# Contrast adjustment on one core: the first store in three pieces beside the loads, and a quarter of the fourth store on another queue

## The chip, the core and the metric

The kernel runs on one core of one Trainium2 chip. The metric is the device time of one execution in microseconds (us); the median of several runs counts.

## The reference

For each image and colour channel (48 planes of 512 x 512 float32 numbers) the mean is taken, and every number is moved away from it by a factor of 1.5 and clipped to 0..1:

```
mean = np.mean(x, axis=(2, 3), keepdims=True)
return np.clip(mean + factor * (x - mean), 0, 1).astype(np.float32)
```

50.33 MB are read and 50.33 MB are written, once each.

## The kernel before

The input is seen as 6 tiles of 128 rows with `ROW` = 16384 numbers (64 KB) each, 8 MB a tile. One plane fills 16 rows, so a tile holds 8 planes. A ring of three such tiles lies in the core's memory (`BUFS` = 3): tile t uses slot t % 3, and load 3 can only start when store 0 has left slot 0, load 4 when store 1 has landed, load 5 when store 2 has.

What is done for a tile:

- **load** (L77): SyncE's queue (SPq in the profile) brings the tile in. Tile 0 comes in three parts (1, 3 and 4 MB), tile 2 in two (7.25 MB and a tail of 0.75 MB, `TAIL`), the others whole.
- **sum_up** (L96) with **add** (L84): row sums. ScalarE runs a copy in place that also sums (L88); for tiles 0 to 2 VectorE sums the first 4352 columns (`SUM`, L91) and ScalarE the rest. For tiles 3 to 5 ScalarE does it alone. Tile 0 is summed by halves.
- **clip** (L101): TensorE multiplies the sums by `blockw` (L105), which adds the 16 rows of a plane and scales, so `bias` holds each row's shift. VectorE then does two operations in place: multiply and add (L108), then clip to 0..1 (L111). Given `cuts`, it does so piece by piece.
- **store** (L80): stores of tiles 0 to 2 go out on ScalarE's queue (ACTq), those of tiles 3 to 5 on SyncE's.

Each queue issues its instructions in the order of the program, and a DMA that waits holds up what is queued behind it on that engine. The order is written out by hand (`manual_schedule`, L115 to L141). On SyncE: the loads of tiles 0, 1 and 2, then load 3 (waiting for store 0), load 4 (store 1), load 5 (store 2), then stores 3, 4 and 5. On ScalarE: the sums of tile 0, the sum of tile 1, store 0 in two pieces (1 MB and 7 MB), the sum of tile 2, store 1, store 2, the sums of tiles 3, 4 and 5. On VectorE: the sums and clips in the order of the tiles. A dependency put in by hand (L125) makes the first piece of store 0 wait for the large part of load 2.

Of the kernel before, what the change touches and what calls it, by code (L numbers as in the profile page):

```python
# [1 line left out]

# [4 lines left out]


P = 128  # L10
ROW = 16384
HALF = ROW // 2
BUFS = 3
SHORT = 2048
SUM = 4352
TAIL = 1536


@with_exitstack
def kernel(  # L20
    ctx: ExitStack,
    tc: tile.TileContext,
    x: bass.AP,
    factor: float,
    out: bass.AP,
):

    nc = tc.nc  # L30
    f32 = mybir.dt.float32
    Alu = mybir.AluOpType
    Act = mybir.ActivationFunctionType

    B, C, H, W = x.shape
    n_img, n_pix = B * C, H * W
    ppi = n_pix // ROW
    per_tile = P // ppi
    n_tiles = n_img // per_tile
    assert ppi * ROW == n_pix and per_tile * n_tiles == n_img  # L40

    factor = float(factor)
    wconst = (1.0 - factor) / float(n_pix)

    x_f = x.rearrange("b c h w -> (b c h w)")
    out_f = out.rearrange("b c h w -> (b c h w)")

    def dram(ap, t, c0=0, c1=ROW):
        return bass.AP(tensor=ap.tensor, offset=t * P * ROW + c0, ap=[[ROW, P], [1, c1 - c0]])

    consts = ctx.enter_context(tc.tile_pool(name="consts", bufs=1))
    xpool = ctx.enter_context(tc.tile_pool(name="xpool", bufs=1))
    small = ctx.enter_context(tc.tile_pool(name="small", bufs=1))
    psum = ctx.enter_context(tc.tile_pool(name="psum", bufs=1, space=bass.MemoryType.PSUM))


    sums = small.tile([P, 4 * n_tiles], f32, name="sums")
    bias = psum.tile([P, n_tiles], f32, name="bias")

    blockw = consts.tile([P, P], f32, name="blockw")  # L60
    blocks = blockw.rearrange("p (a b) -> p a b", b=ppi)
    nc.gpsimd.memset(blockw, wconst)  # L62
    for base, step in ((0, -ppi), (ppi - 1, ppi)):
        nc.gpsimd.affine_select(  # L64
            out=blocks,
            in_=blocks,
            compare_op=Alu.is_ge,
            fill=0.0,
            base=base,
            pattern=[[step, per_tile], [0, ppi]],  # L70
            channel_multiplier=1 if step < 0 else -1,
        )


    ring = xpool.tile([P, BUFS, ROW], f32, name="ring")

    def load(t, c0=0, c1=ROW):  # L77
        return nc.sync.dma_start(out=ring[:, t % BUFS, c0:c1], in_=dram(x_f, t, c0, c1))  # L78

    def store(t, c0=0, c1=ROW):  # L80
        queue = nc.scalar if t < BUFS else nc.sync
        return queue.dma_start(out=dram(out_f, t, c0, c1), in_=ring[:, t % BUFS, c0:c1])  # L82

    def add(t, col, c0, c1, c2):  # L84
        xt = ring[:, t % BUFS, :]
        own = sums[:, 4 * t + col : 4 * t + col + 2]
        part = xt[:, c1:c2]
        nc.scalar.activation(out=part, in_=part, func=Act.Copy, accum_out=own[:, 0:1])  # L88
        if c0 == c1:
            return [own[:, 0:1]]  # L90
        nc.vector.tensor_reduce(  # L91
            out=own[:, 1:2], in_=xt[:, c0:c1], axis=mybir.AxisListType.X, op=Alu.add
        )
        return [own[:, 0:1], own[:, 1:2]]

    def sum_up(t):  # L96
        if t == 0:
            return add(t, 0, 0, SUM, HALF) + add(t, 2, HALF, HALF + SUM, ROW)
        return add(t, 0, 0, SUM if t < BUFS else 0, ROW)

    def clip(t, parts, *cuts):  # L101
        xt = ring[:, t % BUFS, :]
        shift = bias[:, t : t + 1]
        for k, part in enumerate(parts):
            nc.tensor.matmul(shift, blockw, part, start=k == 0, stop=k == len(parts) - 1)  # L105
        for c0, c1 in zip((0, *cuts), (*cuts, ROW)):
            part = xt[:, c0:c1]
            nc.vector.tensor_scalar(  # L108
                out=part, in0=part, scalar1=factor, scalar2=shift, op0=Alu.mult, op1=Alu.add
            )  # L110
            nc.vector.tensor_scalar(  # L111
                out=part, in0=part, scalar1=0.0, scalar2=1.0, op0=Alu.max, op1=Alu.min
            )

    with tc.manual_schedule():  # L115
        load(0, 0, SHORT)
        load(0, SHORT, HALF)
        load(0, HALF, ROW)
        load(1)
        most = load(2, 0, ROW - TAIL)  # L120
        load(2, ROW - TAIL, ROW)
        clip(0, sum_up(0), SHORT)
        parts = sum_up(1)
        first = store(0, 0, SHORT)
        tc.add_manual_dep(  # L125
            first.ins,
            most.ins.name,
            mybir.DependencyInfo(mybir.DependencyClass.Sync, mybir.DependencyReason.DATA),
            reason="the first store follows the loads",
        )  # L130
        store(0, SHORT, ROW)
        clip(1, parts)
        parts = sum_up(2)
        store(1)
        clip(2, parts)
        store(2)
        for t in range(BUFS, n_tiles):
            load(t)
        for t in range(BUFS, n_tiles):
            clip(t, sum_up(t))  # L140
            store(t)  # L141


# [1 line left out]
_INS = ['x', 'factor']  # L145
_OUTS = [((16, 3, 512, 512), 'float32')]

_NUMBERS = {'factor': 1.5}


# [26 lines left out]
```

## Time and profile before

| | us |
|---|---|
| median of 3 runs | 241.26 |
| lowest, highest of the runs | 241.06, 244.25 |
| the profiled execution, its own time | 242.66 |
| span of that execution in the profile | 240.9 |
| VectorE busy, in the span | 123.6 |
| ScalarE busy, in the span | 70.8 |
| share of the 16 DMA engines, SyncE's queue (q1) | 73.9% |
| share of the 16 DMA engines, ScalarE's queue (q10) | 24.4% |

One execution was profiled. Its times are counted from the first instruction of the span. DVE is VectorE, ACT is ScalarE, SP is SyncE; SPq and ACTq are these engines as issuers of DMAs. "Landing" is the end of a transfer as its semaphore shows it. In the windows, the columns after the stretch and its length are the busy us of PE, PEld, DVE, ACT and POOL with their instructions, then TensorE's clock, the mean busy share of the DMA engines, and the GB/s moved. In the timeline, a line gives start, duration, engine, source line and operation, and in brackets the idle time before it.

### The profile page before, as it was taken

The page shows a single profiled execution, that of the slowest core. Times are in us where ns is not written, and L with a number is a line of the kernel's source. Part 1 is how long each engine was busy: PE and PEld are TensorE (multiplying, and loading weights), DVE is VectorE, ACT ScalarE, POOL GpSimd, SP SyncE. Part 2 cuts the span into 40 slices and gives each one's busy share as a digit, 9 for nine tenths or more (in the row PEclk, how much of TensorE's full clock was granted, in tenths as well). Part 3 has the DMA queues.
Part 4 walks back from the last instruction along what each step waited for, and adds up shares of the span by engine and source line. Part 5 has one row for each costly group of instructions (what it writes and reads, how often), then busy time and mean ns, then how long its engine had stood idle before and what let it go on. Part 6 is the DMA issues. An engine that isn't in the chain of part 4 may idle for free.

```text
span 240.9 us, 167 instructions
## 1 busy us (share of the span) xinstructions
PE 6.3 (3%) x22; PEld 5.4 (2%) x22; DVE 123.6 (51%) x18; ACT 70.8 (29%) x15; POOL 1.1 (0%) x7
## 2 busy tenths in 40 slices
PE   0010100010001000000000000000000000000000
PEld 0010100010000000000000000000000000000000
DVE  0072899949998995000000059930089949950000
ACT  2052300960790000000009930029907950000000
POOL 1000000000000000000000000000000000000000
DMA  7999989979999899999999999889899898989894
GB/s 297 411 430 441 511 348 506 473 335 404 501 457 457 348 348 435 435 435 435 424 446 413 446 413 457 381 326 522 348 348 522 348 522 348 522 348 511 359 511 185
DMA packets 2304, 100.66 MB, mean 418 GB/s; under 512 B 256, under 2 KB 256, under 8 KB 384
## 3 DMA queue, kind: packets, MB, share of 16 engines
q1 hardware_dynamic: 1728, 75.50, 73.9%
q10 hardware_dynamic: 576, 25.17, 24.4%
HBM read 50.33 MB, written 50.33 MB: 418 GB/s over the span
## 4 chain that ended last, share of the span: by engine, by line
DMA 54%; ACT 16%; DVE 14%; another core or an unknown queue 3%; SPq 1%; PE 0%; issue 0%; ACTq 0%
DMA ring<-in_x_dram 45%; ACT ring L88 16%; DMA out_dram<-ring 9%; DVE ring L108 7%; DVE ring L111 7%; SPq L78 1%; PE bias L105 0%; ACTq L82 0%; ACTq L172 0%
## 5 line engine op out<-in xcount | busy, mean ns | idle before, releaser
L88 ACT ACTIVATE ring<-ring 128x16384 f32<-128x16384 f32 (+2 forms) x7 | 68.8, 9834 | 124.5 <-DMA ring<-in_x_dram 124.5
L108 DVE TENSOR_SCALAR ring<-ring,bias 128x16384 f32<-128x16384 f32 (+2 forms) x7 | 52.8, 7538 | 72.5 <-PE bias L105 71.7
L111 DVE TENSOR_SCALAR ring<-ring 128x16384 f32<-128x16384 f32 (+2 forms) x7 | 52.3, 7475 | 0.2
L91 DVE TENSOR_REDUCE sums<-ring 128x1 f32<-128x4352 f32 x4 | 18.7, 4683 | 18.0 <-DMA ring<-in_x_dram 18.0
L105 PE MATMUL bias<-sums,blockw 128*128 128x1 f32 x22 | 6.3, 360 | 190.5 <-ACT ring L88 186.0
L105 PEld LDWEIGHTS bias<-sums,blockw 128*128 128x128 f32 x22 | 5.4, 313 | 191.2 <-ACT ring L88 169.9
L88 ACT ACT_TABLE_LOAD x1 | 1.3, 1283 | 0.8 <-PEq L158 0.8
L88 ACT ACTIVATION_READ_ACCUMULATOR ring<-ring 128x1 f32 x7 | 1.3, 186 | 0.0
L64 POOL TENSOR_SCALAR_AFFINE_SELECT blockw<-blockw 128x128 f32<-128x128 f32 x2 | 0.7, 340 | 0.1
L62 POOL MEMSET blockw<- 128x128 f32 x1 | 0.2, 204 | 0.3 <-POOLq L158 0.3
L158 POOL MEMSET const-bfloat16-1.0<- 128x1 bf16 x1 | 0.1, 101 | 0.0
L158 POOL MEMSET const-uint8-127<- 128x1 uint8 x1 | 0.1, 101 | 0.0
L158 POOL MEMSET const-float32-0.0<- 128x1 f32 x1 | 0.1, 98 | 0.3 <-issue 0.3
L158 POOL MEMSET const-float32-1.0<- 128x1 f32 x1 | 0.1, 98 | 0.0
## 6 DMA issues: line engine op xcount, KB each, us to landing
ring<-in_x_dram SPq DMA_DIRECT2D x1, 7424.0 KB, 56.6
out_dram<-ring ACTq DMA_DIRECT2D x1, 7168.0 KB, 20.7
ring<-in_x_dram SPq DMA_DIRECT2D x1, 4096.0 KB, 20.9
ring<-in_x_dram SPq DMA_DIRECT2D x1, 3072.0 KB, 11.7
ring<-in_x_dram SPq DMA_DIRECT2D x1, 1024.0 KB, 4.9
out_dram<-ring ACTq DMA_DIRECT2D x1, 1024.0 KB, 4.3
ring<-in_x_dram SPq DMA_DIRECT2D x1, 768.0 KB, 58.0
ring<-in_x_dram SPq DMA_DIRECT2D x4, 40.7
```

Of the source, the lines that this page charges most:

```text
L62: nc.gpsimd.memset(blockw, wconst)
L64: nc.gpsimd.affine_select(out=blocks, in_=blocks, compare_op=Alu.is_ge, fill=0.0, base=base, pattern=[[step, per_tile], [0, ppi]], channel ...
L78: return nc.sync.dma_start(out=ring[:, t % BUFS, c0:c1], in_=dram(x_f, t, c0, c1))
L88: nc.scalar.activation(out=part, in_=part, func=Act.Copy, accum_out=own[:, 0:1])
L91: nc.vector.tensor_reduce(out=own[:, 1:2], in_=xt[:, c0:c1], axis=mybir.AxisListType.X, op=Alu.add)
L105: nc.tensor.matmul(shift, blockw, part, start=k == 0, stop=k == len(parts) - 1)
L108: nc.vector.tensor_scalar(out=part, in0=part, scalar1=factor, scalar2=shift, op0=Alu.mult, op1=Alu.add)
L111: nc.vector.tensor_scalar(out=part, in0=part, scalar1=0.0, scalar2=1.0, op0=Alu.max, op1=Alu.min)
L158: nc = _bacc.Bacc("TRN2", target_bir_lowering=False, num_devices=1)
```

## The change

- Load 2 comes in one part; the dependency of the first store on it is taken out.
- Tile 0 is clipped in three pieces (2048, 6144 and 8192 columns; 8, 24 and 32 KB a row), and each piece is stored on ScalarE's queue.
- The order on ScalarE changes: all three pieces of store 0 come before the sum of tile 1, and store 1 before the sum of tile 2.
- Tile 3 is clipped in two pieces (4096 and 12288 columns). The first, a quarter, is stored from ScalarE's queue ahead of the sum of tile 4; the rest stays on SyncE's queue behind load 5.

```diff
-TAIL = 1536
+QUARTER = ROW // 4
...
-    def store(t, c0=0, c1=ROW):
-        queue = nc.scalar if t < BUFS else nc.sync
-        return queue.dma_start(out=dram(out_f, t, c0, c1), in_=ring[:, t % BUFS, c0:c1])
+    def store(queue, t, c0=0, c1=ROW):
+        queue.dma_start(out=dram(out_f, t, c0, c1), in_=ring[:, t % BUFS, c0:c1])
...
-        most = load(2, 0, ROW - TAIL)
-        load(2, ROW - TAIL, ROW)
-        clip(0, sum_up(0), SHORT)
-        parts = sum_up(1)
-        first = store(0, 0, SHORT)
-        tc.add_manual_dep(
-            first.ins,
-            most.ins.name,
-            mybir.DependencyInfo(mybir.DependencyClass.Sync, mybir.DependencyReason.DATA),
-            reason="the first store follows the loads",
-        )
-        store(0, SHORT, ROW)
-        clip(1, parts)
-        parts = sum_up(2)
-        store(1)
-        clip(2, parts)
-        store(2)
+        load(2)
+        clip(0, sum_up(0), SHORT, HALF)
+        store(nc.scalar, 0, 0, SHORT)
+        store(nc.scalar, 0, SHORT, HALF)
+        store(nc.scalar, 0, HALF, ROW)
+        for t in range(1, BUFS):
+            clip(t, sum_up(t))
+            store(nc.scalar, t)
         for t in range(BUFS, n_tiles):
             load(t)
-        for t in range(BUFS, n_tiles):
+        clip(BUFS, sum_up(BUFS), QUARTER)
+        store(nc.scalar, BUFS, 0, QUARTER)
+        store(nc.sync, BUFS, QUARTER, ROW)
+        for t in range(BUFS + 1, n_tiles):
             clip(t, sum_up(t))
-            store(t)
+            store(nc.sync, t)
```

## The prediction

> **What bounds the kernel now.** I read the page first, then the chain of work that ended last, then busy time by windows, then the timeline of the stretch that is edited.
>
> The page's slices and packet line:
>
> ```profile
> DMA  7999989979999899999999999889899898989894
> DMA packets 2304, 100.66 MB, mean 418 GB/s; under 512 B 256, under 2 KB 256, under 8 KB 384
> ```
>
> The 16 DMA engines are busy in nearly every slice, while VectorE is busy for 51% of the span and ScalarE for 29%. The chain of waits agrees: it runs from transfer to transfer.
>
> ```profile
> 60.10 20.70 DMA out_dram<-ring
> ...
> 80.89 45.76 DMA ring<-in_x_dram
> ...
> 158.81 23.32 DMA ring<-in_x_dram
> ```
>
> The reader should see that load 3 leaves at 80.89, as the first store lands at 80.80, and that it takes 45.76 us because store 1 runs beside it: sharing costs a transfer time but wastes no bytes. How fast the bytes move is in the windows (last columns: DMA share, GB/s):
>
> ```profile
> 0.00:2.00 2.00, 0.00 (x0) 0.00 (x0) 0.00 (x0) 1.20 (x1) 1.09 (x7) 1.00 0.17 25
> 58.00:64.00 6.00, 0.00 (x0) 0.00 (x0) 5.96 (x2) 2.55 (x1) 0.00 (x0) 1.00 1.09 459
> 84.00:92.00 8.00, 0.00 (x0) 0.00 (x0) 7.97 (x2) 0.00 (x0) 0.00 (x0) 1.00 1.01 336
> 92.00:156.00 64.00, 0.59 (x2) 0.50 (x2) 16.51 (x3) 13.95 (x2) 0.00 (x0) 1.00 1.00 433
> 156.00:164.00 8.00, 0.00 (x0) 0.00 (x0) 2.78 (x1) 2.82 (x1) 0.00 (x0) 1.00 0.98 393
> 176.00:182.00 6.00, 0.00 (x0) 0.00 (x0) 6.00 (x1) 0.00 (x0) 0.00 (x0) 1.00 1.02 350
> 182.00:238.00 56.00, 0.58 (x2) 0.50 (x2) 28.71 (x4) 13.95 (x2) 0.00 (x0) 1.00 0.99 431
> 238.00:240.90 2.90, 0.00 (x0) 0.00 (x0) 0.00 (x0) 0.00 (x0) 0.00 (x0) 1.00 0.00 0
> ```
>
> Loads and stores mixed (92 to 156) give 433 GB/s, stores alone (182 to 238) 431. At 433, 100.66 MB take 232.5 us; the span is 240.9, so 8.4 us are lost. Each window's loss is its length times (1 - rate/433): 1.9 us at the start, 1.8 at 84 to 92, 0.7 at 156 to 164, 1.2 at 176 to 182, 2.9 at the end; sum 8.5. Start and end stay. So 3.7 us is all that any new order of these bytes can win, and an added loss must be a new stretch in which the engines starve or run slowly.
>
> **The change part by part.** The stretch that is edited first:
>
> ```profile
> 28.05 1.29 DVE L108 TENSOR_SCALAR ring<-ring,bias 128x2048 f32<-128x2048 f32 x1 [0.68 <-PE bias L105]
> 29.38 1.23 DVE L111 TENSOR_SCALAR ring<-ring 128x2048 f32<-128x2048 f32 x1
> 30.52 7.68 DVE L108 TENSOR_SCALAR ring<-ring,bias 128x14336 f32<-128x14336 f32 x1
> 38.24 7.63 DVE L111 TENSOR_SCALAR ring<-ring 128x14336 f32<-128x14336 f32 x1
> ...
> 59.63 1.55 ACTq L82 DMA_DIRECT2D out_dram<-ring  x2
> ```
>
> The first piece is ready at 30.6 and leaves at 59.63, held by the wait on load 2.
>
> *VectorE.* From 2048 and 14336 columns, the first operation costs 0.227 us + 0.520 ns a column, the second 0.160 us + 0.521 ns. One cut more costs 0.39 us. The pieces of tile 0 are ready at 30.6, 37.4 (6144 columns: 3.42 + 3.36) and 46.3. Tile 3's cut makes its end 159.2 instead of 158.8, but that store lies behind load 5 on SyncE's queue until about 182: nothing. Its quarter is ready at 141.3 + 2.36 + 2.29 = 146.0.
>
> *Issues.* There are 17 DMAs instead of 16: load 2 loses one, store 0 and store 3 gain one each. An issue takes 0.33 to 1.08 us of its queue, hidden under the transfers queued before it; bare, it would be that.
>
> *ScalarE's queue, which now waits for VectorE.* Queued behind store 0's third piece is tile 1's sum; its pass starts at 42.03 today and would start at 46.3 + 0.4 to 1.1 = 46.7 to 47.4. The matmul and VectorE's clip of tile 1 wait for it: 10.42 to the sum's end, 1.1 to the clip (52.41 to 53.53), 17.5 for the clip, so store 1 leaves at 75.8 to 76.5 instead of 71.11. Tile 2's sum now stands behind store 1: 10.4 more, 1.1, 17.5, and store 2 leaves near 105.5 instead of 93.93. What hides this: loads 0 to 2 and store 0 are 33.55 MB, 77.5 us at 433, so the engines have work until 1.9 + 77.5 = 79.4. Store 1 needs about 1 us from issue to first bytes (the first load is issued at 0.80, and 0 to 2 moves 25 GB/s), so 1.9 to 2.6 us are spare. Store 2 joins behind store 1, whose landing releases load 4 at 119.6: 14 us spare. With the cover gone each us late is a us of idle engines.
>
> *Load 1 and load 2.* Store 0 now shares the engines with them. Load 1 can be late by 4.7 us free (its reader is held until 46.7). Load 3 still waits for the end of store 0, which is the end of the same 33.55 MB: near 80, as now. Removing the wait on load 2's large part and its separate 0.75 MB tail moves nothing else.
>
> *How the sharing starts.* A queue that joins a running one has two rows. The old first piece joined at 60 us beside the end of load 2: 459 GB/s at 58 to 64, no loss. Load 3 joined store 1 near 84: 1.8 us lost. The new join, near 32, is the old piece in direction and size, but the other queue has megabytes left, as near 84. Bounds 0 to +1.8 (less than 0 is excluded, that stretch runs at 426 or more already); between rows that are equally near I take the middle, +0.9.
>
> *The quarter of store 3.* 2 MB, 4.8 us of the engines, leaves ScalarE's queue at 146 behind store 2. Today store 2 lands at about 158.8 and releases load 5, with load 4 ending at 161.15 and store 3 behind load 5. So the engines run dry there, 0.7 us lost. The quarter fills this. Bounds 0 to -0.7; I take -0.7, as 4.8 us of work lies ready.
>
> *The tail.* The quarter goes ahead of load 5's last packets, so load 5 lands at 182.13 + 4.8 - 0.7 = 186.2. From landing to the issue of store 5 take the row of today, 214.29 - 182.13 = 32.2, plus 1 for first bytes: 33.2. The work queued meanwhile is 6 MB of store 3 and 8 MB of store 4, 14.5 + 19.4 = 33.9 (today 38.7). 0.7 us is spare, where 5.5 was: cost 0, up to +1 if load 5's last engine is late. Store 4 leaves near 195 for a need at 200: nothing.
>
> Sum: +0.9 - 0.7 + 0 = +0.2. The profiled execution took 242.66 (span 240.9 and 1.76 around it), so it would take 242.9. It lies 1.4 above the median of 241.26 of the runs; the median plus 0.2 gives 241.5.
>
> **Two rules weighed.** The row for small transfers here is 459 GB/s while the old 1 MB piece ran. The Trainium skill, "DMA: Bandwidth & Descriptors", section "Bandwidth", gives 341 GB/s for a lone 1 MB transfer and wants at least 1 MiB; it speaks against cutting the store, and by it the first piece would cost 1.05 MB/341 - 1.05 MB/433 = +0.65 us (an estimate), where the row beside other work says 0. The row for two queues is 433 GB/s at 92 to 156 against 431 from one queue. The same page, section "Issuing engines are not separate DMA queues", says a second issuing engine saves issue time only; by it the quarter on ScalarE's queue is worth about 0, and what the trace adds is the order behind load 5 that a second queue escapes.
>
> **The rivals.**
> 1. *The bytes set the end, and join and filled gap nearly cancel:* 240.6 to 242.4, likeliest 241.5. For it: 64 us of mixed traffic at 433. Chance 0.48.
> 2. *The early join costs the full 1.8 us and the gap is not filled:* slower, 241.26 + 1.8 = 243.1. It decides as soon as the join costs more than the filled gap gives, 0.7. For it: 84 to 92; against: 58 to 64. Chance 0.20.
> 3. *Store 5 becomes late:* if load 5's landing slips by one 64 KB packet of every engine (19.4/8 = 2.4 us), the 0.7 spare leaves 1.7: 243.0. Against: all engines have equal bytes before load 5. Chance 0.12.
> 4. *The stalls go:* the gap is filled, the new join is free, and load 3, joining a queue already mixed, no longer stalls: 241.26 - 0.7 - 1.8 = 238.8. Against: store 1 runs there alone as before. Chance 0.15.
> 5. *The wait on ScalarE's queue dries the engines:* store 1 over 5 us later than worked out, past 81; then 2 to 4 us idle, some 246 at the worst. Against: the spare 1.9 to 2.6. Chance 0.05.
>
> **How the numbers follow.** 241.5 is the first case. 239.5 to 244.2 takes in the first three and most of the fourth, leaving out half of it (0.08), the fifth (0.05) and 0.05 of the second and third beyond 244.2. About 2% is what a measurement can tell from no change: under 236.4 lies beyond even the 3.7 us (237.6) but for noise, 0.02; over 246.1 the worst of the fifth and double mishaps, 0.06; between them 0.92.
>
> **What would show it.** Right: stores on ScalarE's queue at about 30.7, 37.4 and 46.3; tile 1's sum at 47; store 1 at 76; load 3 still issued at 79 to 82; 156 to 164 near 433; store 5 issued near 218.5; last store about 19.4 us. Wrong: a window under 400 GB/s between 30 and 50 above 1.8 us of loss; engines idle before store 1; a gap before store 5; load 3 issued far from 80, which would say that the queues do not share as I take it.

## The result and the profile after

The changed kernel takes 240.26 us (median; 239.29 to 240.85), the kernel before, in a larger set of runs, 241.58 us (240.79 to 244.28). The ratio is 0.9928, 95% interval 0.9904 to 0.9951: 1.7 us gained (1.2 to 2.3). The ratio is taken over the runs; the two medians lie 1.3 us apart, which is inside its interval. The forecast was 241.5, a gain of nothing. The time lies inside the range of 239.5 to 244.2, but the interval leaves no doubt of a gain, and the +0.2 of the sum pointed the other way.

The profiled execution of the changed kernel took 239.29 us, with a span of 237.5, against 242.66 and 240.9. It is the fastest of its runs, so a difference of these two profiles shows places, not sizes. The page's slices and packet line:

```profile
DMA  7999989999999998989898998989997999999894
DMA packets 2448, 100.66 MB, mean 424 GB/s; under 512 B 272, under 2 KB 272, under 8 KB 272
```

The same bytes move, at 424 GB/s instead of 418. The windows of the prediction were 6 to 8 us long. That is too short: 16 rows of 64 KB are 1 MB, and they enter or leave such a window almost together, so a window of 6 us swings by 100 GB/s or more. (In the changed kernel 176 to 182 shows 350 GB/s with no packet slowed.) Longer windows are better, though by the same reckoning 1 MB is still some 90 GB/s in 12 us and 30 in 34. Before:

```profile
28.00:64.00 36.00, 1.03 (x5) 0.93 (x4) 32.77 (x7) 12.87 (x3) 0.00 (x0) 1.00 1.01 433
80.00:92.00 12.00, 0.00 (x0) 0.00 (x0) 11.97 (x2) 0.00 (x0) 0.00 (x0) 1.00 1.09 399
92.00:150.00 58.00, 0.59 (x2) 0.50 (x2) 10.54 (x2) 13.95 (x2) 0.00 (x0) 1.00 1.00 433
150.00:184.00 34.00, 0.59 (x2) 0.50 (x2) 16.95 (x3) 15.80 (x3) 0.00 (x0) 1.00 1.01 414
```

After:

```profile
28.00:64.00 36.00, 1.01 (x4) 0.93 (x4) 28.52 (x8) 10.32 (x2) 0.00 (x0) 1.00 1.01 424
80.00:92.00 12.00, 1.02 (x4) 0.93 (x4) 4.62 (x2) 6.37 (x2) 0.00 (x0) 1.00 1.03 448
92.00:150.00 58.00, 0.59 (x2) 0.50 (x2) 23.21 (x5) 13.95 (x2) 0.00 (x0) 1.00 1.00 434
150.00:184.00 34.00, 0.59 (x2) 0.50 (x2) 16.61 (x4) 14.51 (x3) 0.00 (x0) 1.00 0.98 424
```

By the windows the early pieces lose 0.7 us at 28 to 64 (36 x (1 - 424/433)) and win at 80 to 92, and the handover from load 4 to load 5 and on to store 3 (150 to 184) runs faster. The trace's records of single packets, one for each row of a transfer on one of the 16 engines, free this from the swing of the windows. A 64 KB row at full speed takes 2.42 us on its engine. "Lost time" below is the length of a stretch less the time that the bytes moved in it take at that speed on 16 engines. By it, 28 to 64 loses 1.1 us in the changed kernel and 0.2 before, 80 to 92 loses nothing after and 2.0 us before, and 150 to 190 nothing after and 2.3 us before.

The issue of store 5 and the waits of SyncE's queue (total, number, longest) show the end of the program, before and after:

```profile
214.29 0.33 SPq L82 DMA_DIRECT2D out_dram<-ring  x1
...
SPq L172 <- DMA out_dram<-ring: 25.2, 2, 19.3
```

```profile
215.58 0.33 SPq L81 DMA_DIRECT2D out_dram<-ring  x1
...
SPq L165 <- DMA out_dram<-ring: 20.6, 1, 20.6
```

Before, at the end of its program, SyncE waits first for store 4 and then 19.3 us for store 5, which had been queued since 214.29. After, store 5 is issued (215.58) and SyncE waits for it alone, 20.6 us: the spare time before store 5 is used up, as the prediction said. Both store 5 and the landing of load 5 came some 3 us earlier than forecast (215.58 against 218.5, 183.44 against 186.2).

### The profile page after: what moved, and what is told of

Read it like the earlier page. It is cut to its first block, busy times and chain, and to the rows that moved or that the text cites. A ratio compares the mean times of both kernels' runs of the same rounds, so it can differ in the third digit from the quotient of the medians.

```text
span 237.5 us, 176 instructions
## 1 busy us (share of the span) xinstructions
PE 6.1 (3%) x22; PEld 5.4 (2%) x22; DVE 124.2 (52%) x22; ACT 70.8 (30%) x15; POOL 1.1 (0%) x7
## 4 chain that ended last, share of the span: by engine, by line
DMA 38%; DVE 24%; another core or an unknown queue 16%; ACT 10%; PE 1%; SPq 1%; issue 0%; ACTq 0%; DVEq 0%
DMA ring<-in_x_dram 20%; DMA out_dram<-ring 18%; DVE ring L107 11%; DVE ring L110 11%; ACT ring L87 10%; DVE sums L90 2%; PE bias L104 1%; SPq L78 1%; ACTq L81 0%; ACTq L165 0%; DVEq L107 0%
## 5 line engine op out<-in xcount | busy, mean ns | idle before, releaser
L107 DVE TENSOR_SCALAR ring<-ring,bias 128x16384 f32<-128x16384 f32 (+5 forms) x9 | 53.2, 5911 | 73.2 <-PE bias L104 73.2
L110 DVE TENSOR_SCALAR ring<-ring 128x16384 f32<-128x16384 f32 (+5 forms) x9 | 52.6, 5849 | 0.3
L104 PE MATMUL bias<-sums,blockw 128*128 128x1 f32 x22 | 6.1, 359 | 191.9 <-ACT ring L87 190.7
```

The lines of the kernel that those rows point to most:

```text
L107: nc.vector.tensor_scalar(out=part, in0=part, scalar1=factor, scalar2=shift, op0=Alu.mult, op1=Alu.add)
L110: nc.vector.tensor_scalar(out=part, in0=part, scalar1=0.0, scalar2=1.0, op0=Alu.max, op1=Alu.min)
```

## The experiments

Every ratio is to the kernel before, on the same chip. Theory G, with which they began: the gain is the hole in which load 5 waits, filled by the quarter. Rival J: it is the loss at 84 to 92, removed by the early pieces.

**One part alone.** The pieces only (e1_pieces_only, against the changed kernel):

```diff
-        clip(BUFS, sum_up(BUFS), QUARTER)
-        store(nc.scalar, BUFS, 0, QUARTER)
-        store(nc.sync, BUFS, QUARTER, ROW)
-        for t in range(BUFS + 1, n_tiles):
+        for t in range(BUFS, n_tiles):
```

> The changed kernel with the quarter undone: store 3 leaves whole on SyncE's queue behind load 5. Theory G (the gain is the gap at 156 to 164, which the quarter fills): the gain is gone, the time is that of the kernel before, within 0.4 us, and the window 156 to 164 is again below 410 GB/s. Rival J (the gain is the stall at 84 to 92, which goes when the first store is spread beside the loads): the whole gain of about 1.7 us (0.7%) stays, and 84 to 92 runs near 430. If both count, about 1 us of gain stays.

Measured: 0.999 (0.9954 to 1.0026), median 242.66. The profiled execution took 241.43 and is one of the four fastest of its twelve, so its windows show a better execution than the median. The quarter only, in the kernel before (e2_quarter_only):

```diff
-        for t in range(BUFS, n_tiles):
+        clip(BUFS, sum_up(BUFS), ROW // 4)
+        nc.scalar.dma_start(out=dram(out_f, BUFS, 0, ROW // 4), in_=ring[:, 0, 0 : ROW // 4])
+        store(BUFS, ROW // 4, ROW)
+        for t in range(BUFS + 1, n_tiles):
```

> The kernel before with the quarter alone: tile 3 is clipped in two pieces and its first quarter is stored from ScalarE's queue. Theory G: 0.7 to 1.7 us faster than before, with 156 to 164 near 433 GB/s. Rival J: no change within 0.4 us, and 84 to 92 is again near 336 GB/s.

Measured: 0.9906 (0.9872 to 0.9941), median 240.58, runs from 240.18 to 240.77. The wait alone taken out (e3_no_wait):

```diff
-        tc.add_manual_dep(
-            first.ins,
-            most.ins.name,
...
-            reason="the first store follows the loads",
-        )
```

> The kernel before without the first store's wait on load 2; the two pieces of store 0 stay behind the sum of tile 1, so they leave near 52.5 us instead of 59.6. Theory G: no change within 0.4 us, since store 0, load 3, store 2 and load 5 end where they did. Rival J: part or all of 1.7 us gained, since the two queues are mixed before load 3 joins.

Measured: 1.0005 (0.9972 to 1.0038). The two pieces left at 41.90 and 45.80 us and not near 52.5: ScalarE's queue issued them while the pass of tile 1's sum (41.89 to 52.1) was still running. And the kernel before for a second profile:

> The kernel before, unchanged, for a second profiled execution. If the slow windows at 84 to 92 and 176 to 182 belong to the order of the transfers (theories G and J), they stand at the same places again. If they are chance stalls of single executions (rival S), they stand elsewhere or are absent, and the time of this execution moves with their sum. The ratio to the kernel before is 1 within 0.3%.

Measured: 0.9993 (0.9961 to 1.0025); 80 to 92 runs at 382 GB/s and 150 to 184 at 409, so both losses belong to the order of the transfers. The quarter alone carries the whole gain, with 80 to 92 as slow as before; J falls as the cause of the gain, though the interval of e1 still leaves room for up to 1.1 us from the pieces. The windows of e1 and e2:

```profile
28.00:64.00 36.00, 1.01 (x4) 0.93 (x4) 28.52 (x8) 10.32 (x2) 0.00 (x0) 1.00 1.02 426
80.00:92.00 12.00, 1.02 (x4) 0.93 (x4) 4.62 (x2) 6.22 (x2) 0.00 (x0) 1.00 1.03 445
...
150.00:184.00 34.00, 0.59 (x2) 0.50 (x2) 16.30 (x3) 17.03 (x3) 0.00 (x0) 1.00 0.98 405
```

```profile
28.00:64.00 36.00, 1.01 (x4) 0.93 (x4) 32.77 (x7) 12.80 (x3) 0.00 (x0) 1.00 1.01 433
80.00:92.00 12.00, 0.00 (x0) 0.00 (x0) 11.96 (x2) 0.00 (x0) 0.00 (x0) 1.00 1.08 399
...
150.00:184.00 34.00, 0.59 (x2) 0.50 (x2) 16.74 (x3) 13.95 (x2) 0.00 (x0) 1.00 0.99 428
```

**Queue, cut, size or moment?** The quarter's store on SyncE's queue instead of ScalarE's (f1_cut_same_queue, against e2):

```diff
-        nc.scalar.dma_start(out=dram(out_f, BUFS, 0, ROW // 4), in_=ring[:, 0, 0 : ROW // 4])
+        store(BUFS, 0, ROW // 4)
```

> The kernel before with tile 3 clipped and stored in a quarter and three quarters, but both stores on SyncE's queue behind load 5. The quarter alone on ScalarE's queue gave the whole gain (0.9906). Theory Q (the second queue gives it: the quarter runs while load 5 waits and beside load 5): the gain is gone, ratio 0.997 to 1.002. Rival C (cutting store 3 gives it, since 48 KB rows follow load 5 without the slow last packets seen at 176 to 182): about 1.1 us of gain stays, ratio near 0.995.

Measured: 0.9979 (0.9948 to 1.001), 150 to 184 at 403 GB/s: no gain clear of noise. The queue matters, not the cut. An eighth instead of the quarter (f2_eighth; the half, f3_half, has `ROW // 2` at the same places; both against e2):

```diff
-        clip(BUFS, sum_up(BUFS), ROW // 4)
-        nc.scalar.dma_start(out=dram(out_f, BUFS, 0, ROW // 4), in_=ring[:, 0, 0 : ROW // 4])
-        store(BUFS, ROW // 4, ROW)
+        clip(BUFS, sum_up(BUFS), ROW // 8)
+        nc.scalar.dma_start(out=dram(out_f, BUFS, 0, ROW // 8), in_=ring[:, 0, 0:ROW // 8])
+        store(BUFS, ROW // 8, ROW)
```

> As the quarter alone, with an eighth (1 MB, 2.4 us of the engines) on ScalarE's queue. It covers the hole in which load 5 waits (0.1 to 1.2 us in four profiles) but is used up by about 168, long before load 5 ends. Theory H (the hole is the gain): about as good as the quarter, ratio 0.990 to 0.993. Rival T (the slow handover from load 5 to store 3 at 176 to 182, about 1.1 us in each of four profiles, goes because another queue has work beside load 5): that handover is slow again and half the gain or less is left, ratio 0.995 to 0.998.

Measured: 0.9928 (0.9899 to 0.9957), 150 to 184 at 447 GB/s. As good as the quarter within the intervals, as theory H expects. But load 5 also ended at full speed, although the eighth was over by then (its last row ended at 169.9): the slow handover went too, without work beside it, which neither theory had foreseen.

> As the quarter alone, with a half (4 MB) on ScalarE's queue. Load 5 shares the engines with all of it and lands about 9.7 us later than before less what the holes gave (2.2), near 189; behind it lie only 9.7 + 19.3 = 29 us of stores against 33.2 us from load 5's landing to the first bytes of store 5. All theories: the engines run dry before store 5 for about 4 us, and the time is 1 to 2.5 us over the kernel before, ratio 1.004 to 1.010.

Measured: 1.0117 (1.0069 to 1.0165), a little more than forecast: slower by 2.8 us. Here the cover of the prediction is gone. Load 5 lands at 190.7, store 5 leaves at 222.87, and the engines lose 6.0 us before it (about 4 were expected):

```profile
214.00:222.00 8.00, 0.00 (x0) 0.00 (x0) 7.96 (x2) 0.00 (x0) 0.00 (x0) 1.00 0.32 139
```

The last quarter of the row instead of the first, ready 13 us later (f4_last_quarter, against e2):

```diff
-        clip(BUFS, sum_up(BUFS), ROW // 4)
-        nc.scalar.dma_start(out=dram(out_f, BUFS, 0, ROW // 4), in_=ring[:, 0, 0 : ROW // 4])
-        store(BUFS, ROW // 4, ROW)
+        clip(BUFS, sum_up(BUFS), 3 * ROW // 4)
+        nc.scalar.dma_start(out=dram(out_f, BUFS, 3 * ROW // 4, ROW), in_=ring[:, 0, 3 * ROW // 4:ROW])
+        store(BUFS, 0, 3 * ROW // 4)
```

> As the quarter alone, but the quarter on ScalarE's queue is the last of tile 3, ready at 159.2 instead of 146, so that it is not there while load 5 waits for store 2 and runs only beside load 5. Theory H (the hole while load 5 waits): the gain is gone, ratio 0.997 to 1.002. Rival T (the handover from load 5 to store 3): half of the gain or more stays, ratio 0.991 to 0.996, with no slow packets as load 5 ends.

Measured: 1.0003 (0.9969 to 1.0036), 150 to 184 at 400 GB/s. Work that joins as load 5 starts, instead of lying ready, gains nothing. The time is that of theory H, but the end of load 5 is that of rival T: its last rows ran at full speed, and the loss stood at its start, where the first rows took 3.1 us (median) and the next two 2.8 instead of 2.42. The quarter was issued at 159.21, and its first row began at 163.2.

**Where store 3 begins.** In f1 and, the half apart, in all kernels without gain the store behind load 5 begins at column 0, in those with gain it does not. Two kernels part this from the queue. Both parts on SyncE's queue, the three quarters first (g1_rest_first, against f1):

```diff
-        store(BUFS, 0, ROW // 4)
         store(BUFS, ROW // 4, ROW)
+        store(BUFS, 0, ROW // 4)
```

> The kernel before with both parts of store 3 on SyncE's queue, the three quarters from column 4096 first, then the quarter. The slow last packets of load 5 went in the kernels whose store behind load 5 begins at column 2048 or 4096 (the eighth, the quarter) and stayed where it begins at column 0 (whole, and cut on the same queue). Theory A (where the store behind load 5 begins decides): no slow packets as load 5 ends, and a ratio of 0.993 to 0.997. Theory B (work of the second queue while load 5 starts decides): the slow packets stay, ratio 0.997 to 1.002.

Measured: 1.0006 (0.9972 to 1.0039). The last quarter, but clipped first and so ready near 146, on ScalarE's queue (g2_tail_early, against f4):

```diff
-        for c0, c1 in zip((0, *cuts), (*cuts, ROW)):
+        pieces = list(zip((0, *cuts), (*cuts, ROW)))
+        for c0, c1 in pieces[::-1] if t == BUFS else pieces:
```

> As the quarter alone, but it is the last quarter of the row, clipped first, so that it leaves ScalarE's queue near 145; what stays behind load 5 on SyncE's queue begins at column 0. Theory A: the slow last packets of load 5 are back and half the gain is left, ratio 0.994 to 0.998. Theory B: the full gain, ratio 0.988 to 0.994, with no slow packets from 156 to 185.

Measured: 0.9915 (0.9886 to 0.9944), 150 to 184 at 429 GB/s. Theory B holds in both; the column is without effect. A tiny piece, 512 columns (g3_tiny, against e2):

```diff
-        clip(BUFS, sum_up(BUFS), ROW // 4)
-        nc.scalar.dma_start(out=dram(out_f, BUFS, 0, ROW // 4), in_=ring[:, 0, 0 : ROW // 4])
-        store(BUFS, ROW // 4, ROW)
+        clip(BUFS, sum_up(BUFS), 512)
+        nc.scalar.dma_start(out=dram(out_f, BUFS, 0, 512), in_=ring[:, 0, 0:512])
+        store(BUFS, 512, ROW)
```

> As the quarter alone, with 512 columns (0.25 MB, 0.6 us of the engines) on ScalarE's queue. Theory B, if the work has to last until load 5's first packets: it is used up about 158 to 160 for most engines, so half the gain or less, ratio 0.995 to 0.999. Theory A: the slow last packets are gone as the store behind load 5 begins at column 512, ratio near 0.994.

Measured: 0.9961 (0.9929 to 0.9993), about half of the gain, as B expects; the interval reaches from a fifth of a us to the whole gain and also holds A's 0.994. The changed kernel for a second profile:

> The changed kernel, unchanged, for a second profiled execution. Theory B: again no loss from 150 to 185 and a last store that starts late by a few tenths of a us. The ratio to the kernel before is 0.990 to 0.995. Whether the loss at 84 to 92, absent from its first profile, comes back is not foretold by either theory; if it does, it was chance.

Measured: 0.9887 (0.9848 to 0.9927), with 80 to 92 at 451 GB/s again: that loss does not come back.

**The slow last packets.** The records of single packets show how long the last row of load 5 takes on each of the 16 engines, and the lost time as defined above, in us. "To the end" runs to the end of the span and holds some 1.2 us behind the last packet in every kernel.

| kernel | last rows of load 5 start (us) | duration, median (us) | lost, 150 to 190 | lost, 150 to the end | ratio |
|---|---|---|---|---|---|
| before | 177.3 to 177.8 | 3.61 | 2.3 | 4.0 | 1 |
| e4, before again | 176.1 to 177.3 | 3.57 | 1.2 | 3.9 | 0.9993 |
| e1, pieces only | 176.2 to 176.9 | 3.55 | 2.3 | 3.8 | 0.999 |
| e3, no wait | 176.3 to 177.7 | 3.10 | 0.8 | 3.9 | 1.0005 |
| f1, cut, same queue | 176.3 to 177.4 | 3.64 | 1.3 | 3.7 | 0.9979 |
| g1, rest first, same queue | 177.8 to 178.4 | 3.79 | 2.4 | 4.1 | 1.0006 |
| f4, last quarter, late | 181.8 to 183.9 | 2.42 | 1.9 | 4.2 | 1.0003 |
| h4, pieces held | 176.4 to 179.0 | 3.85 | 1.8 | 5.2 | 1 |
| h1, store 3 waits for load 5 | 177.5 to 178.8 | 2.42 | 2.9 | 4.3 | 1.0002 |
| g3, 512 columns | 176.6 to 177.7 | 2.52 | 0.4 | 2.5 | 0.9961 |
| f2, an eighth | 178.8 to 179.5 | 2.42 | 0.0 | 1.6 | 0.9928 |
| g2, last quarter, early | 180.9 to 182.0 | 2.42 | 0.0 | 2.0 | 0.9915 |
| e2, a quarter | 181.1 to 182.0 | 2.42 | 0.0 | 1.8 | 0.9906 |
| after | 179.8 to 180.7 | 2.42 | 0.0 | 1.8 | 0.9928 |

The reader should see that work lying ready removes the whole loss around load 5, and that the kernels without gain lose 3.7 to 5.2 us from 150 on, whichever way it falls, against 1.6 to 2.0 with an eighth or more lying ready (2.2 to 3.2 in g4, h2, h3, i1 and i2). Where less was lost around load 5 (e3, e4, f1), the engines finished out of step instead: the last rows of the program ended over 2.1 us in e4 (237.4 to 239.5) and over 0.9 us in the first profile of the same kernel.

h1_store3_waits asks whether store 3, queued behind load 5, is needed for this:

```diff
-            load(t)
+            last = load(t)
...
-            store(t)
+            s = store(t)
+            if t == BUFS:
+                tc.add_manual_dep(
+                    s.ins,
+                    last.ins.name,
...
+                    reason="store 3 follows load 5",
+                )
```

> The kernel before, with store 3 made to wait until load 5 has landed, so that no store is queued behind load 5. Theory S (store 3, queued behind load 5, slows load 5's last packets): load 5 lands about 1.1 us earlier after load 4 (about 19.8 instead of 21 us), and the 1.5 to 2 us between its landing and store 3's first bytes make the time 0.5 to 1 us longer than before. Rival L (load 5 slows by itself at its end when it began alone): it lands 21 us after load 4 as before, and the time is 1.5 to 2.5 us longer.

Measured: load 5's rows run at full speed to the end, and it lands 20.35 us after load 4 (181.60 - 161.25 by the starts of the sums) instead of 20.97; the time is 1.0002 (0.9972 to 1.0031). So the slow rows need store 3 behind them: theory S, though the landing moved by 0.6 us and not by 1.1. The 0.5 to 1 us that the gap before store 3 should have cost is not told from nothing by the time, whose interval reaches 0.75 us; in the packet records 150 to 190 loses 2.9 us instead of 2.3, since some 2 us without packets stand where the slow rows were.

**The tail and the pieces again.** The changed kernel with an eighth (h2_after_eighth) and with three sixteenths (h3_after_3_16, `3 * ROW // 16`):

```diff
-QUARTER = ROW // 4
+QUARTER = ROW // 8
```

> The changed kernel with an eighth of tile 3 on ScalarE's queue instead of a quarter. If the changed kernel ends on the wait for store 5 (0.4 to 1.2 us of idle engines near 216 in two profiles), an eighth leaves 2.4 us more work to cover it: 0.3 to 1 us faster than the changed kernel, ratio to before 0.986 to 0.990, no idle near 216. If that wait costs nothing, the ratio is that of the changed kernel or worse, 0.990 to 0.994.

> The changed kernel with three sixteenths. As the eighth: if the wait for store 5 costs time, ratio 0.986 to 0.990; if not, that of the changed kernel.

Measured: 0.9873 (0.9844 to 0.9902) and 0.9862 (0.9834 to 0.9889), on a chip on which the changed kernel had not run. To settle it, the changed kernel and three sixteenths on one chip (i1_after_beside, i2_3_16_beside):

> The changed kernel once more, on the same chip as the next. If the wait for store 5 costs it time, it is 0.3 to 0.8 us slower than three sixteenths; if not, the two medians lie within 0.2 us.

> The changed kernel with three sixteenths, on the same chip. If the wait for store 5 costs the quarter time: median 0.3 to 0.8 us below the changed kernel's; if not, within 0.2 us.

Measured: 0.9923 (0.9896 to 0.9951) and 0.992 (0.9894 to 0.9945), medians 240.81 and 240.54. The two medians lie 0.3 us apart and the intervals cover each other: no better version is shown, and what the wait for store 5 costs the quarter is under what these runs resolve. In the profiles the engines lose 0.2, 0.9 and 1.2 us before store 5 with the quarter, 0.0 and 0.3 with three sixteenths, nothing with the eighth. Last, the three pieces with the hold of before (h4_pieces_held, against the kernel before):

```diff
-        clip(0, sum_up(0), SHORT)
+        clip(0, sum_up(0), SHORT, HALF)
...
-        store(0, SHORT, ROW)
+        store(0, SHORT, HALF)
+        store(0, HALF, ROW)
```

> The kernel before with tile 0 clipped and stored in three pieces, but still held until load 2's large part has landed. If the size of the pieces ahead of store 1 removes the loss at 84 to 92, that window runs above 400 GB/s, and the ratio is 0.992 to 0.997 if the loss comes back nowhere else. If sharing the engines with load 1 and 2 removes it, the window is again near 340 and the ratio is 1 within 0.3%.

Measured: 1.0 (0.9974 to 1.0027), with 80 to 92 at 410 GB/s and 84 to 92 at 352. The cut alone does not remove that loss (2.0 us by the packets), and neither does sharing from 41.9 us on in two pieces (e3, 393 GB/s at 80 to 92, 1.7 us). In all seven profiles with three pieces that leave from 30.5 us on it is gone (440 to 451 GB/s, lost time 0.0, against 366 to 415 GB/s and 1.7 to 2.2 us in the thirteen others). Those seven also have load 2 in one part and store 1 ahead of the sum of tile 2, and no run parts these from the early pieces.

## Why the prediction was wrong, point by point

*What bounds the kernel: right.* The DMA engines do, the 433 GB/s of mixed traffic held (434 after), and the ceiling of 3.7 us bounded the gain.

*VectorE and the issues: right.* The pieces left ScalarE's queue from 30.55 on, and the clip of tile 0 ended at 46.1:

```profile
29.29 1.23 DVE L110 TENSOR_SCALAR ring<-ring 128x2048 f32<-128x2048 f32 x1
30.43 3.42 DVE L107 TENSOR_SCALAR ring<-ring,bias 128x6144 f32<-128x6144 f32 x1
30.55 15.99 ACTq L81 DMA_DIRECT2D out_dram<-ring  x3
33.89 3.36 DVE L110 TENSOR_SCALAR ring<-ring 128x6144 f32<-128x6144 f32 x1
37.16 4.48 DVE L107 TENSOR_SCALAR ring<-ring,bias 128x8192 f32<-128x8192 f32 x1
41.68 4.43 DVE L110 TENSOR_SCALAR ring<-ring 128x8192 f32<-128x8192 f32 x1
46.02 4.68 DVE L90 TENSOR_REDUCE sums<-ring 128x1 f32<-128x4352 f32 x1
46.59 10.23 ACT L87 ACTIVATE ring<-ring 128x12032 f32<-128x12032 f32 x1 [20.49 <-DVE ring L110]
```

*The new wait on ScalarE's queue: right.* The last line's bracket is that wait: the sum of tile 1 starts at 46.59, now released by VectorE and not by load 1. Store 1 left at 75.66 (forecast 75.8 to 76.5), store 2 at 105.12 (105.5), load 3 at 81.84 (near 80). The cover held; rival 5 did not happen.

*The join: half right.* The early join costs 0.7 us at 28 to 64, close to the +0.9 taken. What the step missed is that the loss at 80 to 92 then goes, which it left to rival 4. 12 us at about 445 instead of 392 GB/s (the means of the two groups of profiles) are 1.5 us, so by the windows the pieces should win 0.7. By the packets, 28 to 64 and 80 to 92 together lose 1.1 to 1.3 us in the seven profiles with the pieces and 2.1 to 2.8 in the thirteen others, which is 1.2 us won. By the time they win 0.2 us, with an interval from 0.6 lost to 1.1 gained (0.999): too small to be told from nothing, and why it is not more stays open.

*The quarter: the step that failed.* It was priced at 0 to -0.7 from the hole at 156 to 164 alone. The profile showed two losses around load 5, 0.7 at 156 to 164 and 1.2 at 176 to 182, and the sum took the second as a fixture, without asking what ends there: the last rows of load 5, with store 3 next on the same queue. The quarter removes both, 0.7 + 1.2 = 1.9 by the prediction's own windows and 2.3 by the packets (1.1 before 168 us, 1.2 after), and measured alone it gives 2.3 us (0.9906; 1.4 to 3.1), in the changed kernel 1.7. With -1.9 in place of -0.7 and the pieces at nothing the sum would have said 239.4 by the median then known, or 239.7 by the median of the larger set.

The starts of the sums of tiles 4 and 5 show it. Before, and with the quarter alone:

```profile
161.18 13.86 ACT L88 ACTIVATE ring<-ring 128x16384 f32<-128x16384 f32 x1 [20.56 <-DMA ring<-in_x_dram]
...
182.15 13.86 ACT L88 ACTIVATE ring<-ring 128x16384 f32<-128x16384 f32 x1 [7.03 <-DMA ring<-in_x_dram]
```

```profile
161.79 13.86 ACT L88 ACTIVATE ring<-ring 128x16384 f32<-128x16384 f32 x1 [21.09 <-DMA ring<-in_x_dram]
...
184.74 13.86 ACT L88 ACTIVATE ring<-ring 128x16384 f32<-128x16384 f32 x1 [9.00 <-DMA ring<-in_x_dram]
```

4.8 us of other work went ahead, and load 5 is only 2.6 us later. Behind it the span is shorter by 4.7 (238.8 - 184.74 = 54.1 against 240.9 - 182.15 = 58.75). The difference, 2.1 us, is the fall of the span from 240.9 to 238.8.

*The tail: right in kind.* Spare before, used up after; the 0 to +1 us allowed for it covers the 0.2 to 1.2 lost in three profiles, and the times do not resolve it. The landing of load 5 in its sum, 186.2, was 2.8 us too late (183.44) through the same step: it took 0.7 off the 4.8 us of the quarter, where 2.2 went with the quarter alone (182.15 + 4.8 - 184.74). The half shows what lies beyond: +2.8 us.

*The rule on small transfers.* The 341 GB/s that the prediction takes from the Trainium skill, "DMA: Bandwidth & Descriptors", section "Bandwidth", stand there for loads issued from GpSimd. The first piece of 1 MB was in the kernel before as well, so its price was no price of the change. No run has a lone 1 MB store. At 28 to 64 the slow packets were the 64 KB rows of the loads, and every row of the store's pieces ran at full speed.

*The rule on two queues.* f1 and e2 differ in the queue of one store alone: 0.9979 against 0.9906, some 1.8 us, where the issue itself takes 0.34 us. The Trainium skill, "DMA: Bandwidth & Descriptors", section "Issuing engines are not separate DMA queues", allows a second queue the saved issue time only. The measurement decides: the bytes move no faster, but a queue keeps its order, and a second one has work ready where the first must wait.

*What stays open.* Why load 5's last rows are slow with store 3 behind them if the second queue was empty when load 5 began and stayed so; an eighth, whose last row ended at 169.9, is enough to prevent it, and so is a quarter that comes late (f4), though there the first rows are slow instead. Why the loss at 80 to 92 goes in the kernels with the early pieces. And why the kernels with at least an eighth of tile 3 lying ready on the second queue vary less (the changed kernel by 1.6 us over its 21 runs, the kernel before by 3.5 over its 21).

## What to carry to other kernels

Where transfers bound a kernel and every slice looks busy, list each stretch below the full rate, ask what starts or ends there, and price all that an edit could touch, also a stretch that it is not meant for. At a place where the next load on one queue waits for a store, a small piece of another store that lay ready on the second queue was worth more here than the hole; it had to be there before the load started, and it had to leave enough work to cover the last tile's compute. A window as short as a few rows of a transfer shows no rate; the packets' own durations do.

## What the runs showed of the hardware that was not expected

- The last 64 KB row of load 5 took 3.6 us (median; 3.1 in e3) instead of 2.42, on every one of the 16 engines, when a store followed it on the same queue and the other queue stayed empty from the load's start on (seven profiles); with the store held back until the landing it took 2.42.
- 1 MB on the second queue at the right moment gained 1.7 us (0.9928), 0.25 MB about half of that (0.9961), and 2 MB that came 13 us later nothing (1.0003).
- Beside 64 KB rows of a load, pieces of 8, 24 and 32 KB a row ran at 424 GB/s over 36 us, against 433 with load 1 and load 2 almost alone; the time went to the load's rows.
- A DMA whose queue joined a running one had its first row late: load 3 after 3.5 to 5.2 us from its issue, the early first piece of store 0 after 3.5 to 4.1. Where the engines had run dry (load 5 before, issued at 158.81) it was 1.0.
